# Seven products for the second part of layer 0's feed-forward network, with sums of weights made in DRAM during the convolutions

## The chip, the core and the metric

The kernel runs on one core of a Trainium2 chip, in one launch. The metric is the device time of one execution in microseconds; "before" and "after" are medians of several runs, and beside them stands one profiled execution of each kernel, from whose trace all views are taken.

## The reference

Two layers of a hybrid decoder over 512 tokens of width 1024, all in float32. Layer 0 is a Conformer convolution module and a SwiGLU feed-forward network, layer 1 sliding-window attention and another SwiGLU network. Cut to what matters here:

```python
def swiglu_ffn(x, w_up, w_down):              # w_up 1024 x 5632, w_down 2816 x 1024
    gate, up = jnp.split(x @ w_up, 2, axis=-1)
    return (jax.nn.silu(gate) * up) @ w_down

for l in range(2):
    if l == 0:   # causal depthwise convolution, 31 taps, per channel
        h = h + conformer_conv(rmsnorm(h, norm_mix[0]), ...)
    else:
        h = h + attention(rmsnorm(h, norm_mix[1]), k_shared, v_shared, ...) @ w_o
    h = h + swiglu_ffn(rmsnorm(h, norm_ffn[l]), ffn_w_up[l], ffn_w_down[l])
return rmsnorm(h, norm_final)
```

## The kernel before

Activations lie transposed, channels on the 128 partitions and tokens along the row. Products keep float32 accuracy by splitting each operand into a high and a low part of the faster float32r kind: a product is then three matmuls, high x high, high x low and low x high (`mm3`, L349 to L351). The high part of a weight chunk is a ScalarE copy (`whi`, L263), the low part a VectorE subtraction (`wlo`, L266). In the first products of layer 0 plain float32 is used instead (L347), with chunks that are not split.

Weights come in chunks of 128 x 1024 float32 (512 KB), in the fixed order of a list, `PLAN`. SyncE loads each into a `raw` buffer (L239, seven buffers, at most nine chunks ahead of use), and it is split at most three ahead of use. A buffer is free again when its split is done.

The hidden width of a feed-forward network is cut into eleven pairs of 256 columns of gate and 256 of up. **Layer 0's network** runs in two parts: pairs 0 to 4 (first part) separately for the two halves of the tokens, as each half leaves the convolution module, and pairs 5 to 10 (second part) for all 512 tokens at once. In the first part the second half's products use a form with two matmuls (`twin`, L381, L382). In the second part each pair takes four up chunks of 8 blocks of 128 x 128, each a `mm3` over 512 tokens; VectorE, ScalarE and GpSimd then form silu(gate) * up (L634 to L637), which is split for the down projection.

**Layer 1's network** takes ten of its eleven pairs by *seven products*: a pair's up weights and the rows x are cut into 2 x 2 blocks, and the four blocks of the result come from seven block products of 256 tokens (A11 B11, S1 T1, S2 T2, A12 B21, S3 T3, S4 B22, A22 T4) in place of eight. S1 to S4 are sums of weight blocks, T1 to T4 sums of blocks of rows. Its down projections go the same way ("low", L844). The results are gathered by ScalarE and VectorE (L784 to L796) and gated (L802 to L804, the last on GpSimd). T1 to T4 are made by GpSimd (L726) and split.

**The sums of weights** are made in DRAM, one chunk each, by `prepare` (60 of them): SyncE copies one block to a place in DRAM (L255), and GpSimd issues a transfer that adds another block onto it (L259). A sum that builds on another waits for that one to land, and what stands behind it in GpSimd's queue waits too. `share` says how many of these steps are taken per chunk used: 1/3 in the first part of the second token half, 1/2 in layer 0's second part, then 1, then 1/3.

**The convolution module** also works in two halves of 256 tokens. Its 31 taps per channel are divided: VectorE does some (L951), for the rest ScalarE multiplies (L943) and GpSimd adds (L944), and GpSimd adds both shares into `y` (L955). From y follow squares and sums (L1000), mean and variance, a spread over partitions (L1031), `z` (L1045), and the second projection on TensorE (L347). The taps of half 1 run beside the projections of half 0. The reciprocal root `rs` of the next norm is a GpSimd instruction (L474), and its spread (L496) stands in TensorE's queue among the first pairs' products.

In between SyncE and TensorE make a table for the attention bias: a small product at L1101, written 128 times over to DRAM (`fd`, 3 MB, L1104), read back in parts as bias tiles (L1195).

A scheduler orders each engine's instructions within the program's dependences; every engine works through its own list in that order. `issue_after` ties an instruction behind another one.

## Time and profile before

| | before |
|---|---|
| median of 3 runs | 1062.3 us (1059.25 to 1062.88) |
| the profiled execution | 1060.15 us |
| its span in the profile | 1058.4 us |
| TensorE's clock as granted, mean | 0.996 |
| TensorE busy | 1046.2 us, 99% of the span |
| VectorE, ScalarE, GpSimd busy | 737.6, 576.6, 437.8 us |
| moved by DMA | 211.04 MB |

All times in views are microseconds from the span's start, unless marked ns. Matmuls are pipelined, so "busy" of TensorE (PE) is not TensorE at its peak, and the mean duration of a matmul is longer than the distance from one to the next. PEld is its weight load, DVE is VectorE, ACT ScalarE, POOL GpSimd, SP SyncE. L259 is line 259 of the kernel before. "idle before <- X" is how long an engine stood idle ahead of a group and what ended that.

### The profile page before, as it was taken

To read this page: it belongs to the slowest core of one execution; us is meant where nothing else is said; L and a number is where in the kernel's file an instruction comes from. 1 tells how busy PE (TensorE), PEld (TensorE's weight loads), DVE (VectorE), ACT (ScalarE), POOL (GpSimd) and SP (SyncE) were. 2 spreads that over 40 slices of the span, in tenths; PEclk is the share of its full clock that TensorE was granted. 3 is DMA by queue.
4 is the path that set the end of the run, shared out by engine and by line. 5 is a ranking of instruction groups with operands and counts; after the bars stand their busy time and mean duration, and the time that the engine had idled before them with its cause. 6 is when DMAs were issued, how large, how long until landed. Compare 5 with 4: busy or idle time off the path is not lost.

```text
span 1058.4 us, 16667 instructions
## 1 busy us (share of the span) xinstructions
PE 1046.2 (99%) x6166; PEld 923.3 (87%) x6166; DVE 737.6 (70%) x1163; ACT 576.6 (54%) x1008; POOL 437.8 (41%) x535
## 2 busy tenths in 40 slices
PE   9999999999999999999999999999999999999996
PEld 8888889999988888888888877778989999898995
DVE  3999988977866654454427466678678777868677
ACT  3887897854645423322325465556655555554653
POOL 3999999810333312221124255305242323323131
PEclk9999999999999999999999999999999999999998
DMA  9438045577999996767779876765799565555532
GB/s 354 153 96 98 7 140 199 182 225 218 278 291 293 327 256 183 213 164 192 204 210 247 239 199 172 187 164 170 239 274 305 185 196 174 170 194 183 195 121 80
DMA packets 56606, 211.04 MB, mean 199 GB/s; under 512 B 6891, under 2 KB 13196, under 8 KB 55564
## 3 DMA queue, kind: packets, MB, share of 16 engines
q1 hardware_dynamic: 47164, 177.42, 49.8%
q0 software_dynamic: 8640, 31.46, 16.9%
q8 instruction: 48, 0.79, 0.3%
q10 hardware_dynamic: 720, 1.10, 0.3%
q14 instruction: 34, 0.28, 0.1%
HBM read 204.71 MB, written 68.16 MB: 258 GB/s over the span
## 4 chain that ended last, share of the span: by engine, by line
PE 89%; ACT 4%; issue 2%; POOL 2%; DVE 1%; DMA 1%; SPq 0%; ACTq 0%; POOLq 0%
PE bank L349 19%; PE bank L351 19%; PE bank L350 19%; PE bank L844 9%; PE bank L902 8%; PE bank L381 5%; PE bank L382 3%; ACT pr L943 1%; PE bank L1302 1%; PE bank L1344 1%; PE bank L1331 1%; PE bank L1000 1%; DMA sum<-in_W_dram 1%; POOL pr L944 1%; DMA both<-in_lead_dram 1%
## 5 line engine op out<-in xcount | busy, mean ns | idle before, releaser
L266 DVE TENSOR_TENSOR wlo<-raw,whi 128x1024 fp32r<-128x1024 f32 x231 | 305.8, 1332 | 166.1 <-ACT whi L263 165.1
L263 ACT CAST whi<-raw 128x1024 fp32r<-128x1024 f32 x231 | 241.2, 1049 | 274.8 <-PE bank L350 194.4
L349 PE MATMUL bank<-quad,whi 128*128 128x256 f32 (+1 forms) x976 | 326.9, 336 | 0.0
L350 PE MATMUL bank<-quad,whi 128*128 128x256 f32 (+1 forms) x976 | 326.0, 334 | 0.0
L351 PE MATMUL bank<-quad,wlo 128*128 128x256 f32 (+1 forms) x976 | 326.0, 334 | 0.0
L349 PEld LDWEIGHTS bank<-quad,whi 128*128 128x128 f32 x976 | 185.3, 190 | 19.8 <-issue 1.6
L351 PEld LDWEIGHTS bank<-quad,wlo 128*128 128x128 f32 x976 | 185.3, 190 | 18.8 <-issue 0.6
L350 PEld LDWEIGHTS bank<-quad,whi 128*128 128x128 f32 x976 | 185.4, 190 | 18.4 <-issue 0.2
L944 POOL TENSOR_TENSOR pr<-pr,pr 128x256 f32<-128x256 f32 x208 | 159.0, 798 | 3.8 <-ACT pr L943 3.8
L951 DVE SCALAR_TENSOR_TENSOR bank<-apad,wdw,bank 128x256 f32<-128x256 f32 x248 | 112.3, 484 | 3.3
L943 ACT ACTIVATE pr<-apad,wdw 128x256 f32<-128x256 f32 x208 | 98.2, 501 | 15.4 <-POOL pr L944 13.2
L804 POOL TENSOR_TENSOR up<-up 128x512 f32<-128x512 f32 x20 | 35.4, 1769 | 162.2 <-ACT up L803 162.2
L902 PE MATMUL bank<-quad,w 128*128 128x256 f32 x448 | 98.7, 380 | 0.0
L259 POOL DMA_DIRECT2D sum<-in_W_dram x30 | 25.0, 832 | 174.1 <-DMA sum<-in_W_dram 152.4
L902 PEld LDWEIGHTS bank<-quad,w 128*128 128x128 f32 x448 | 84.9, 190 | 11.8 <-DVE bank L951 0.2
L349 PE MATMUL bank<-rows,whi 128*128 128x256 f32 x320 | 90.8, 284 | 0.5 <-ACT up L788 0.5
L351 PE MATMUL bank<-rows,wlo 128*128 128x256 f32 x320 | 90.6, 283 | 0.0
L350 PE MATMUL bank<-rows,whi 128*128 128x256 f32 x320 | 90.5, 283 | 0.0
L259 POOL DMA_DIRECT2D sum<-sum x30 | 24.7, 823 | 140.7 <-DMA sum<-in_W_dram 128.4
L381 PE MATMUL bank<-quad,whi 128*128 128x512 f32 x212 | 76.0, 398 | 0.0
L349 PEld LDWEIGHTS bank<-rows,whi 128*128 128x128 f32 x320 | 61.4, 192 | 0.9 <-ACT up L788 0.7
L350 PEld LDWEIGHTS bank<-rows,whi 128*128 128x128 f32 x320 | 61.4, 192 | 0.3
(218 smaller groups left out, 1642.9 us busy)
## 6 DMA issues: line engine op xcount, KB each, us to landing
raw<-in_W_dram SPq DMA_DIRECT2D x183, 512.0 KB, 4.2
sum<-in_W_dram SPq DMA_DIRECT2D x60, 512.0 KB, 5.8
raw<-sum SPq DMA_DIRECT2D x60, 512.0 KB, 4.4
sum<-in_W_dram POOLq DMA_DIRECT2D x30, 512.0 KB, 7.0
sum<-sum POOLq DMA_DIRECT2D x30, 512.0 KB, 7.5
w<-in_W_dram SPq DMA_DIRECT2D x14, 512.0 KB, 9.3
fd<-fs SPq DMA_DIRECT2D x1, 3072.0 KB
h<-in_xT_dram SPq DMA_DIRECT2D x8, 256.0 KB, 8.4
```

The costliest lines, as they stand in the source:

```text
L259: nc.gpsimd.dma_start(summed[a], chunk(a, SUMS[a[2]][1]), accum_op=ALU.add, max_dma_last_dim=4096)
L263: on_act = nc.scalar.copy(hi, src).ins
L266: latest[:] = [on_act, lo_engine[0].tensor_sub(lo, src, f32(hi)).ins]
L349: nc.tensor.matmul(out, w[0], x[0], start=start, stop=False, **kw)
L350: nc.tensor.matmul(out, w[0], x[1], start=False, stop=False, **kw)
L351: nc.tensor.matmul(out, w[1], x[0], start=False, stop=stop, **kw)
L381: nc.tensor.matmul(first[2], first[0], first[1], start=start, stop=False)
L844: nc.tensor.matmul(out, x, w[:, ws], start=first and e == 0 and i == 0, stop=e == 1 and i == 2, skip_group_check=True)
L902: mm = nc.tensor.matmul(self.pb[:, w * W2:(w + 1) * W2], w1_of(ct, w, k), x[k] if x else xg[k][:, tok], start=k == 0, stop=k == KT - 1)
L943: on_act = nc.scalar.mul(pr, a[:, j:j + W2], tap(j))
L944: on_pool = nc.gpsimd.tensor_add(pr, acc, pr)
L951: on_dve = nc.vector.scalar_tensor_tensor(yt if i == nd - 1 else c, src, tap(i), c if i else self.shift, op0=ALU.mult, op1=ALU.add)
```

## The change

The six pairs of layer 0's second part (5 to 10) take their up projections by seven products too, from x and bc0 of both halves. The rows' sums T1 to T4 are made from the unsplit rows (`plain` of the first half, and a new `plain1` of the second), by GpSimd, in the first part of the second token half. `seven_pair` serves both layers now; for layer 0 it also multiplies the up half by the norm's factor, and writes into a pool of five buffers (`z0`), whose other tiles are `plain1` and T1 to T3. The down projections of the second part keep their matmuls and come after the six pairs.

The 24 sums of layer 0's pairs (S1 to S4 of six pairs) are made in four batches of six chunks, 3 MB each. The four copies are issued by SyncE behind the loads of the bias table's inputs. The four adds are issued by GpSimd: S1, S3 and S2 tied behind an add of the convolution's half 0, S4 behind one of half 1. Each add is one transfer of 768 rows of 4 KB. S2 adds onto A11 what S1 holds, S4 onto A12 what S2 holds.

Besides, the raw buffers go from seven to six, the first three bias tiles are read behind the six pairs instead of ahead of the first part, and `share` is 1/5 in the six pairs, then 1/2 in their down projections.

```diff
+EARLY_ADDS = {8: "S1", 9: "S3", 13: "S2"}
 def by_seven(layer, pair):
-    return layer == 1 and pair in SEVENS
+    return pair in SEVENS if layer else pair >= HALVES0[1][0]
...
-            r = wpool.tile([P, 1024], F32, tag="raw", name=uid("raw"), bufs=7)
+            r = wpool.tile([P, 1024], F32, tag="raw", name=uid("raw"), bufs=6)
...
+    def blocks_early(name):
+        if name[0] == "S":
+            return early_sums[name]
+        i = CHUNK_AT[EARLY[0] + (name,)]
+        return W[i:i + len(EARLY)].rearrange("u p c -> p u c")
+
+    def copy_early(name):
+        early_sums[name] = dpool.tile([P, len(EARLY), 1024], F32, tag=uid("sum"), name=uid("sum"))
+        for i, u in enumerate(EARLY):
+            summed[u + (name,)] = early_sums[name][:, i]
+        return nc.sync.dma_start(early_sums[name], blocks_early(SUMS[name][0])).ins
+
+    def add_early(name):
+        nc.gpsimd.dma_start(early_sums[name], blocks_early(SUMS[name][1]), accum_op=ALU.add, max_dma_last_dim=4096)
...
         def table_in():
             nc.sync.dma_start(sk, sinks.to_broadcast([P, NH]))
             nc.sync.dma_start(lhs[0:NBUCKET, :], relb)
-            nc.sync.dma_start(oh, onehot)
+            behind = nc.sync.dma_start(oh, onehot).ins
+            for name in ("S1", "S3", "S2", "S4"):
+                with tc.issue_after(behind):
+                    behind = copy_early(name)
...
+            if at_ in EARLY_ADDS:
+                with tc.issue_after(h0.pooled):
+                    add_early(EARLY_ADDS[at_])
...
         job(second, (base, 0), (base + 8, 19), (base + 13, 22), (base + 25, 40), (base + 36, h1.n_steps - early))
+        with tc.issue_after(h1.pooled):
+            add_early("S4")
...
-    def seven_pair(pair, rows, pool, between=None):
-        c = new_gates(pool)
+    def seven_pair(kind, pair, rows, c, between=None):
...
             nc.scalar.activation(gate, gate, AF.Silu)
+            if kind == "up0":
+                nc.vector.tensor_mul(c[:, m, :, 1, :], c[:, m, :, 1, :], rs_bc)
             nc.gpsimd.tensor_mul(gate, gate, c[:, m, :, 1, :])
...
+    class Rows0:
+        def sums(self):
+            b11, b12, b21, b22 = (f[:, j * 4:j * 4 + 4] for j in range(2) for f in self.f)
+            t1 = wpool.tile([P, 4, 256], F32, tag="raw", name=uid("t1"), bufs=6)
+            for n, (name, t, f, a, b) in enumerate((
+                    ("T1", t1, nc.gpsimd.tensor_sub, b11, b12), ("T2", b11, nc.gpsimd.tensor_add, b22, t1),
+                    ("T3", b12, nc.gpsimd.tensor_sub, b22, b12), ("T4", b21, nc.gpsimd.tensor_sub, b11, b21))):
+                f(t, a, b)
+                yield
+                ...
+                split([both[:, e] for e in range(2)], t, name == "T2")
+                yield
...
-    n1 = Next(("ffn0",), x0, bc0, HALF[1])
+    n1 = Next(("ffn0",), x0, bc0, HALF[1], plain=plain1)
+    job(rows0.sums(), (base + 10, 0), (base + 30, 9))
     pw2(h1.z, n1)
     ffn_part(0, 0, x0["ffn0"], HALF[1], n1.rms, twin=True)
...
+    share[0] = 1 / 5
+    lo0, hi0 = HALVES0[1]
+    hid0 = Act(2 * (hi0 - lo0))
+    for pair in range(lo0, hi0):
+        c = seven_pair("up0", pair, rows0, z0.tile([P, 2, 2, 2, 256], F32, tag="z0", name=uid("up"), bufs=5))
+        for m in range(2):
+            split([d.rearrange("p (s q) -> p s q", s=2) for d in hid0[2 * (pair - lo0) + m]], c[:, m, :, 0, :])
...
-        ffn_part(0, 1, x0["ffn0"], ALL, Both(), nxt.on_h)
+        for g in range(2):
+            banks = accs(512)
+            down_group([(("down", 0, kp, g), 2 * (kp - lo0)) for kp in range(lo0, hi0)], lambda kt: hid0[kt], banks)
```

More of the change, by code (lines that the diff above doesn't have):

```diff
@@ L87, in ffn @@
         for pair in range(lo, hi):
-            plan.extend(ups(layer, pair))
+            plan.extend(blocks_of("up0", pair) if by_seven(layer, pair) else ups(layer, pair))
         for g in range(2):
@@ L243, in prepare @@
     def prepare():
-        units = [c[:2] for c in PLAN if is_block(c) and c[2] == "S1"]
+        units = UNITS[len(EARLY):]
         adds, todo, before = [], [], None
@@ L391, in hybrid_trunk @@
     w1 = [None] + [quads.tile([P, 2, KT, P], F32, tag="quad", name=uid("w1")) for _ in range(1, KT)]
-    both = [wpool.tile([P, 1024], F32, tag="raw", name=uid("both"), bufs=7) for _ in range(KT // 2)]
+    both = [wpool.tile([P, 1024], F32, tag="raw", name=uid("both"), bufs=6) for _ in range(KT // 2)]
     x_first = [both[k // 2][:, k % 2 * 512:k % 2 * 512 + 256] for k in range(KT)]
@@ L728, in sums @@
                 both = quads.tile([P, 2, 4, 256], F32R, tag="quad", name=uid("rows"))
-                self.block[name] = [both[:, a] for a in range(2)]
-                split(self.block[name], t, name == "T2")
+                self.block[name] = [[both[:, e, k] for k in range(4)] for e in range(2)]
+                split([both[:, e] for e in range(2)], t, name == "T2")
     def new_gates(pool):
@@ L771, in seven_pair @@
         for n, name in enumerate(SEVEN):
[L772 removed]
+            w = [x.rearrange("p (a k c) -> p a k c", a=2, k=4) for x in get_seven(kind, pair, n)]
             a, b = name.split()
@@ L780, in seven_pair @@
                 for k in range(4):
-                    mm3(r[:, which], [v[:, which, k, :] for v in w], [x[e][:, k, :] for e in range(2)],
+                    mm3(r[:, which], [v[:, which, k, :] for v in w], [x[e][k] for e in range(2)],
                         first and which == 0 and k == 0, which == 1 and k == 3, skip_group_check=True)
@@ L1197, in read_bias, with __init__, step2 @@
                                       ap=[[NH * 3 * P - 1, P], [3 * P, 2], [1, BAND]]))
+    preparing[0], share[0] = prepare(), 1 / 3
+    class Rows0:
+        rms = None
+        def __init__(self, x, h0_, h1_):
+            self.f = h0_, h1_
+            self.block = {f"B{j + 1}{s + 1}": [[x[j * 4 + k][e][:, HALF[s]] for k in range(4)] for e in range(2)]
+                          for j in range(2) for s in range(2)}
+        def step2(self):
+            return bc0
+        def sums(self):
[6 more added lines that the diff above has]
+                yield
+                if n < 3:
+                    both = z0.tile([P, 2, 4, 256], F32R, tag="z0", name=uid("rows"), bufs=5)
+                else:
+                    both = quads.tile([P, 2, 4, 256], F32R, tag="quad", name=uid("rows"))
+                self.block[name] = [[both[:, e, k] for k in range(4)] for e in range(2)]
+                split([both[:, e] for e in range(2)], t, name == "T2")
+                yield
@@ L1199, in hybrid_trunk @@
+    part2 = ExitStack()
+    z0 = part2.enter_context(tc.tile_pool(name="part2", bufs=5))
+    plain1 = z0.tile([P, KT, W2], F32, tag="z0", name=uid("plain1"), bufs=5)
+    n1 = Next(("ffn0",), x0, bc0, HALF[1], plain=plain1)
     base = seen[0]
-    job(chain(*(read_bias(*b) for b in ((0, 0), (0, 1), (1, 0)))), (base, 0), (base + 30, 7))
-    preparing[0], share[0] = prepare(), 1 / 3
-    n1 = Next(("ffn0",), x0, bc0, HALF[1])
+    rows0 = Rows0(x0["ffn0"], plain, plain1)
+    rows0.rms = rows0
```

31 lines of the change are left out of this document (18 added, 13 removed).

## The prediction

> **What bounds the kernel now.** I read the page first (busy shares, the slices, the queues), then TensorE's waits, the windows and the timelines of single engines around the stages that the change touches. A page row gives busy us, share and instructions; a slice is 26.5 us, a digit tenths busy.
>
> ```profile
> span 1058.4 us, 16667 instructions
> ...
> PE 1046.2 (99%) x6166; PEld 923.3 (87%) x6166; DVE 737.6 (70%) x1163; ACT 576.6 (54%) x1008; POOL 437.8 (41%) x535
> ...
> POOL 3999999810333312221124255305242323323131
> DMA  9438045577999996767779876765799565555532
> ```
>
> TensorE waits for nothing worth naming: these are all its waits (us in total, times, longest).
>
> ```profile
> PE bank L434 <- POOL ones_m L431: 1.1, 1, 1.1
> PE bank L890 <- DVE quad L864: 0.9, 2, 0.6
> PE bank L349 <- ACT up L788: 0.5, 1, 0.5
> PE bank L496 <- ACT tmp L482: 0.2, 1, 0.2
> ```
>
> So matmul time taken out shortens the span, unless something makes TensorE wait. GpSimd is idle over most of the span, but not in the convolutions: slices 2 to 7 read 9. The fourth wait, at 179.6 us, is where its lateness reaches TensorE. DMA has room in slices 2 and 3 (4 and 3 tenths) and 5 (none busy).
>
> **What is saved.** Before, a pair of the second part is 4 chunks x 8 blocks x 3 = 96 matmuls of 512 columns; after, 7 products x 8 blocks x 3 = 168 of 256. The first two rows below are the same step of the first and the last pair (five pitches apart), the last two the same step of two neighbouring seven-product pairs of layer 1 (start, duration, instruction).
>
> ```profile
> 381.46 0.69 DVE L636 TENSOR_TENSOR tmp<-bank,rsbc 128x512 f32<-128x512 f32 x1 [0.59 <-PE bank L351]
> 490.26 0.69 DVE L636 TENSOR_TENSOR tmp<-bank,rsbc 128x512 f32<-128x512 f32 x1 [0.59 <-PE bank L351]
> 865.53 0.59 ACT L786 ACTIVATE up<-bank 128x512 f32<-128x512 f32 x1
> 885.69 0.59 ACT L786 ACTIVATE up<-bank 128x512 f32<-128x512 f32 x1
> ```
>
> (490.26 - 381.46) / 5 = 21.76 us now, 885.69 - 865.53 = 20.16 us by seven: 1.60 us a pair, less than the eighth of the columns that goes (a matmul of 256 takes 20.16 / 168 = 0.120 us). Six pairs: **9.6 us saved**. The down projections keep their matmuls.
>
> **What it costs in the stage itself.** Windows give us, then busy (instructions) of PE, PEld, DVE, ACT, POOL, granted clock, DMA share, GB/s; groups give busy us and mean ns.
>
> ```profile
> 290.00:345.00 55.00, 55.00 (x313) 47.55 (x312) 35.92 (x41) 29.06 (x47) 19.78 (x15) 1.00 0.94 290
> 450.00:500.00 50.00, 50.00 (x222) 41.43 (x221) 23.81 (x25) 15.41 (x19) 11.39 (x10) 1.00 0.67 181
> 830.00:890.00 60.00, 60.00 (x425) 56.41 (x424) 44.87 (x50) 32.58 (x42) 17.32 (x14) 1.00 0.57 186
> L266 DVE TENSOR_TENSOR wlo<-raw,whi 128x1024 fp32r<-128x1024 f32 x231 | 305.8, 1332 | 166.1 <-ACT whi L263 165.1
> L263 ACT CAST whi<-raw 128x1024 fp32r<-128x1024 f32 x231 | 241.2, 1049 | 274.8 <-PE bank L350 194.4
> L726 POOL TENSOR_TENSOR quad<-quad,quad x2: 3386/3388/3390, 722.4 to 725.7; 128x1024 f32<-128x1024 f32 x2
> L259 POOL DMA_DIRECT2D sum<-in_W_dram x30: 805/826/1040, 258.7 to 800.9; - x30
> 1015.75 5.52 PE bank L844 x24
> ```
>
> Seven chunks to split a pair are 7 x 1.33 = 9.3 us of VectorE and 7.3 us of ScalarE in 20.2; with evictions and gates some 16 and 13. Layer 1 runs so at 45 of 60 us: hidden; uncovered, 1.33 us a chunk. The four sums of rows (4 x 3.4 us of GpSimd, 4 x 1.05 of ScalarE, 4 x 1.33 of VectorE) and the second half's plain rows (eight ScalarE multiplies) lie in the part before, under TensorE, with 20, 29 and 36 busy of 55: hidden; uncovered, the first T1 product would wait 3.4 us per sum. One raw buffer fewer leaves six, 17 us ahead at 2.9 us a chunk: nothing, and 2.9 us where it ever fails. Layer 1's own sums fall behind by 36/2 - (42/5 + 12/2) = 3.6 of 60; at one in three chunks later on that is 31 us, and the last first-step add is issued at 801 us, the last low products start at 1016: nothing. The bias reads move to the down projections, where DMA was 0.67 busy: nothing.
>
> **What it costs in the convolutions.** The program's order shows four batch copies of 3 MB on SyncE behind the one-hot table and ahead of the first raw loads, and four batch adds on GpSimd's queue: S1 behind the 23rd of the 31 tap adds in the first row below, S3 twelve instructions on, S2 seven after that, S4 sixty behind S2.
>
> ```profile
> 70.11 21.31 POOL L944 TENSOR_TENSOR pr<-pr,pr 128x256 f32<-128x256 f32 x31
> ...
> 103.72 1.41 POOL L955 TENSOR_TENSOR y<-y,pr 128x256 f32<-128x256 f32 x2
> ...
> 178.13 0.71 POOL L474 TENSOR_TENSOR rs<-ms,mhalf 128x2 f32<-128x2 f32 x1
> ...
> 189.83 10.43 POOL L944 TENSOR_TENSOR pr<-pr,pr 128x256 f32<-128x256 f32 x9 [0.61 <-ACT pr L943]
> 110.00:180.00 70.00, 69.75 (x350) 61.71 (x348) 61.91 (x139) 58.30 (x133) 67.85 (x89) 1.00 0.35 121
> 179.62 0.70 PE L496 MATMUL bank<-tmp,ones_m 128*128 128x256 f32 x2 [0.25 <-ACT tmp L482]
> 129.41 1.89 PE L347 MATMUL bank<-z,raw 128*128 128x256 f32 x8
> ```
>
> GpSimd does one such add per 21.31 / 31 = 0.687 us without a gap. S1's turn is 23 adds behind 70.11, at 85.9 us; S3's comes 8.2 us after it, S2's 4.8 us after that, at 98.9 us plus two issues. S2 reads what S1 wrote and so waits for S1's landing. Behind it stand in line: the last two y of half 0 (103.72), on which the statistics, z and the second projection (129.41) hang; all taps of half 1; and the rs at 178.13, whose spread TensorE awaits at 179.62. GpSimd is 67.85 of 70 us busy up to there: what is put in ahead of rs is not made up. Slack: the order puts the spread 18 matmuls later (18 x 0.12 = 2.2 us) and one tap add behind rs (0.7), less the 0.25 waited already: 2.6 us. After 200 us GpSimd is free.
>
> How long is an issue, and when does S1 land?
>
> ```profile
> DMA to landing us min/median/max: 5.1/7.3/9.9
> ...
> q1 hardware_dynamic: 47164, 177.42, 49.8%
> q0 software_dynamic: 8640, 31.46, 16.9%
> 31.56 40.03 SPq L239 DMA_DIRECT2D raw<-in_W_dram  x7
> 73.91 0.34 SPq L1104 DMA_DIRECT2D fd<-fs  x1
> 78.00:82.00 4.00, 4.00 (x20) 3.52 (x19) 4.00 (x11) 3.30 (x8) 4.00 (x7) 1.00 0.89 101
> 102.00:106.00 4.00, 4.00 (x20) 3.54 (x19) 3.09 (x8) 3.55 (x10) 4.00 (x7) 1.00 0.90 100
> 106.00:110.00 4.00, 4.00 (x21) 3.51 (x20) 3.75 (x8) 1.92 (x4) 4.00 (x7) 1.00 0.26 38
> ```
>
> An issue d: 0.83 us for 128 rows (L259, above; min, median and max in ns); a batch has 768. It lies between 0.83 (all fixed) and 6 x 0.83 = 5.0 us (all per row); below 0.83 nothing points. I take 1.5, near the only row there is. The Trainium skill (DMA: Bandwidth & Descriptors, section Anatomy of one DMA) says that many descriptors can be emitted before their number costs; by that d would be 0.83 and the sum below come out 2.0 us lower; no run here shows a large batch.
>
> Copies: q1 moved 177.42 MB in 49.8% of 1058.4 us, 2.97 us per MB, so a 3.15 MB copy takes 9.3 us and four 37: from 32-36 to about 73 us, in DMA's hole. Raw loads wait behind them and are needed at 129: nothing; without that cover, 9.3 us each.
>
> The adds: q0 spent 16.9% of 1058.4 us on 60 adds of 512 KB, 2.98 us each; a batch takes 17.9 us of all engines. But the bias table's write (fd, issued at 73.91) holds 0.89 of the engines until 107 us. Alone S1 would land at 85.9 + d + 17.9 = 105; stretched as the small adds are, 7.3/5.1 = 1.43 times, at 113; at 9.9/5.1 = 1.94 times, at 122. I take 113. S2 lands behind S3, 2 x 17.9 us later, at 149 us; S4's turn is sixty instructions behind S2, 41 us, at 156: no wait.
>
> The sum: S2's turn is at 98.9 + 3.0 = 101.9, it waits 11.1 us; with four issues of 1.5, GpSimd is 17.1 us later at rs; less 2.6, TensorE loses 14.5. 14.5 - 9.6 = **+4.9 us**. On the profiled execution, 1060.15 us (span 1058.4), that is 1065.0; it lay 2.15 us below the median of 1062.3, so I forecast **1067 us**. Bounds of this case: d and landing from (0.83, 110) to (5.0, 118) give delays of 12.8 to 29 us less 2.6, so 1063 to 1079, its middle 1064 to 1073.
>
> **The rivals.**
>
> *S1 lands in time.* If the engines serve the add beside the slow table write, it lands at 104.6 with d = 0.83: the wait is 4.1, the delay 7.4, the loss 4.8, so 4.8 us faster, **1057**; with d = 2, where S2 waits 2.9 us, 1061. For it: the table write moves only 100 GB/s, so its share may be waiting, not moving. Against: 0.89 busy. The case turns to a gain where the delay stays under 12.2 us. Not waiting at all it gives 1053 at d = 0.83.
>
> *GpSimd is held while it issues.* The kernel gives these queues 2048 bytes per partition. If S3's descriptors don't fit beside S1's, GpSimd stands until most of S1 has drained, and S2's until most of S3, another 12 to 18 us: a delay of about 32 us, +20, **1082**. It decides as soon as two batches fill the ring; the small adds before never did. The Trainium skill (Perfetto Trace Analysis, section DMA Instruction — SWDGE (GPSIMD)) says engines begin before the last descriptor is written, the more so where they don't fit in the buffer. No row here shows a full one.
>
> *The seven products don't run at layer 1's pace.* GpSimd's sum adds stand in the same queue as the gates:
>
> ```profile
> POOL sum L259 <- DMA sum<-in_W_dram: 280.8, 48, 31.5
> ```
>
> If such a wait (31.5 us at worst) outlasts the two gate buffers, about 20 us, a pair stalls. Once, on top of the forecast, that is 11 us: **1078**. Against: layer 1 has the same queue and TensorE waited 0.5 us in it.
>
> **How the numbers follow.** The forecast 0.50, S1 in time 0.28, the full ring 0.13, slow products 0.09. A difference under 0.3% (3.2 us) can't be told from none. Faster by more, below 1059.1: about two thirds of S1 in time and a sliver of the forecast's smaller delays, 0.24. Same: the rest of S1 in time and the forecast's lower end, 0.16. Slower: 0.60. The range takes in S1 in time from 1055 and the upper cases up to 1081.
>
> **What would show it.** In the profile after: pair pitch 20.2 us from the first seven-product pair on; a wait of GpSimd at the S2 add for the S1 landing, about 11 us, ending near 113; y of half 0 some 10 to 12 us late; TensorE idle 11 to 15 us in all between 105 and 200 us, none of it later; the four issues 0.8 to 5 us each. Wrong it is if the S2 add finds S1 landed, if GpSimd stands at S3, or if TensorE stalls after 350 us.

## The result: slower by 5%, and the profile after

| | before | changed |
|---|---|---|
| median of the runs beside each other, us | 1062.59 (4 runs, 1059.25 to 1063.28) | 1116.08 (4 runs, 1112.93 to 1121.17) |
| ratio to before, 95% interval | | 1.0514 [1.0469, 1.0560] |
| span of the profiled execution, us | 1058.4 | 1111.1 |

The forecast was 1067 us in a range of 1055 to 1081. The sign was right, the size was not: the change costs 53 us. First the page of the changed kernel (busy us and share, then the 40 slices, 27.8 us each).

```profile
span 1111.1 us, 17707 instructions
...
PE 1044.5 (94%) x6598; PEld 939.1 (85%) x6598; DVE 781.2 (70%) x1203; ACT 615.3 (55%) x1062; POOL 454.2 (41%) x543
...
POOL 3994279794028331222212335522335342314132
PEclk9999579999998999999999999999999999999999
DMA  9999873955588999888997876766689985555542
```

TensorE's busy time is even a little shorter; its idle time grew from 12.2 to 66.6 us. GpSimd, full in slices 2 to 7 before, now has a hole in slices 4 and 5 (digits 4 and 2); TensorE's clock is down in slices 5 and 6 (5 and 7), and the DMA engines read 9 in slices 1 to 4. TensorE's waits say where that arrives (us in total, times, longest):

```profile
PE bank L1024 <- POOL y L979: 40.5, 3, 38.9
PE bank L517 <- ACT tmp L503: 7.0, 2, 3.8
PE bank L913 <- DVE quad L887: 1.9, 2, 1.6
PE bank L403 <- DVE wlo L287: 1.8, 2, 1.0
PE bank L372 <- DVE wlo L287: 1.7, 1, 1.7
```

One wait of 38.9 us for half 0's y, and two of 3 to 4 us at the spreads. GpSimd's own timeline (start, duration, instruction; in brackets the idle time before it and what ended that, "issue" meaning that nothing in the profile did) shows why y is late. L281 is the batch add, in the order S1, S3, S2.

```profile
70.26 15.82 POOL L967 TENSOR_TENSOR pr<-pr,pr 128x256 f32<-128x256 f32 x23
98.31 1.49 POOL L281 DMA_DIRECT2D sum<-in_W_dram  x1 [12.23 <-issue]
...
126.39 1.32 POOL L281 DMA_DIRECT2D sum<-in_W_dram  x1 [18.37 <-issue]
...
146.25 1.17 POOL L281 DMA_DIRECT2D sum<-sum  x1 [13.75 <-issue]
...
149.72 1.16 POOL L979 TENSOR_TENSOR y<-y,pr 128x256 f32<-128x256 f32 x1
...
229.84 1.72 POOL L495 TENSOR_TENSOR rs<-ms,mhalf 128x2 f32<-128x2 f32 x1
```

An issue itself takes 1.2 to 1.5 us, but GpSimd stands 12.2, 18.4 and 13.8 us in front of three of them: 44.4 us. With the four issues (5.2 us) that is 49.6 of the 51.7 us by which rs is late (178.13 before). The first data packet of S1 is at 107.8 us, and each batch then moves for 16 to 18 us: S1 to 125.8, S3 128.5 to 145.6, S2 148.1 to 164.2. GpSimd is let go at S3 and at S2 just when the batch before has drained. These windows (us, then busy of PE, PEld, DVE, ACT, POOL, granted clock, DMA share, GB/s) show what the engines did meanwhile, and the price of standing still:

```profile
86.00:98.00 12.00, 12.00 (x57) 10.58 (x56) 3.06 (x8) 0.51 (x1) 0.08 (x1) 1.00 0.89 98
98.00:108.00 10.00, 8.47 (x38) 6.62 (x38) 6.15 (x14) 6.23 (x14) 9.69 (x13) 1.00 0.89 97
114.00:154.00 40.00, 4.42 (x10) 3.36 (x11) 6.17 (x14) 8.81 (x19) 13.86 (x20) 0.50 0.84 160
343.00:349.00 6.00, 4.65 (x13) 3.89 (x14) 6.00 (x7) 3.70 (x9) 6.00 (x3) 0.50 0.67 207
```

In the first two the table's write is all that moves, at 97 to 98 GB/s, also after S1 has been issued. In the last two the granted clock is 0.50: after these stalls TensorE first ran on at half speed, 5 us of it behind the long one.

The saving is there. The same step of two seven-product pairs of layer 0, four pitches apart:

```profile
452.10 0.59 ACT L807 ACTIVATE up<-bank 128x512 f32<-128x512 f32 x1
532.27 0.59 ACT L807 ACTIVATE up<-bank 128x512 f32<-128x512 f32 x1
```

(532.27 - 452.10) / 4 = 20.04 us a pair, against 21.76 before and 20.16 forecast. By TensorE's marks the 52.7 us of the span come about so, to within half a microsecond: the spread of half 0 is at 232.3 in place of 179.6 (+52.7), the last twin matmul at 422.9 in place of 361.9 (another +8.3), the first attention matmul at 651.8 in place of 598.7 (7.9 back). Two questions, then: what holds GpSimd, and what takes 8 us of the twin part (the first part's second half of the tokens), which I had taken to hide the new work.

### The profile page after: what moved, and what is told of

Its sections match the earlier page's. It is cut to its first block, busy times and chain, and to the rows that moved or that the text cites. A ratio compares the mean times of both kernels' runs of the same rounds, so it can differ in the third digit from the quotient of the medians.

```text
span 1111.1 us, 17707 instructions
## 1 busy us (share of the span) xinstructions
PE 1044.5 (94%) x6598; PEld 939.1 (85%) x6598; DVE 781.2 (70%) x1203; ACT 615.3 (55%) x1062; POOL 454.2 (41%) x543
## 4 chain that ended last, share of the span: by engine, by line
PE 71%; issue 8%; DVE 7%; POOL 7%; ACT 3%; DMA 2%; SPq 0%; DVEq 0%; POOLq 0%; ACTq 0%
PE bank L370 18%; PE bank L372 18%; PE bank L371 18%; PE bank L867 9%; POOL pr L967 4%; DVE bank L975 3%; DMA sum<-in_W_dram 2%; DVE wlo L287 1%; PE bank L402 1%; PE bank L1376 1%; PE bank L1418 1%; PE bank L1405 1%; ACT pr L966 1%; DVE quad L525 1%; PE bank L403 1%
## 5 line engine op out<-in xcount | busy, mean ns | idle before, releaser
L287 DVE TENSOR_TENSOR wlo<-raw,whi 128x1024 fp32r<-128x1024 f32 x249 | 337.3, 1364 | 127.7 <-ACT whi L284 126.0
L284 ACT CAST whi<-raw 128x1024 fp32r<-128x1024 f32 x249 | 259.6, 1048 | 274.0 <-PE bank L371 191.5
L372 PE MATMUL bank<-quad,wlo 128*128 128x256 f32 (+1 forms) x928 | 292.4, 316 | 1.7 <-DVE wlo L287 1.7
L370 PE MATMUL bank<-quad,whi 128*128 128x256 f32 (+1 forms) x928 | 293.0, 317 | 0.0
L371 PE MATMUL bank<-quad,whi 128*128 128x256 f32 (+1 forms) x928 | 292.3, 315 | 0.0
L370 PEld LDWEIGHTS bank<-quad,whi 128*128 128x128 f32 x928 | 177.3, 191 | 12.2 <-issue 1.3
L371 PEld LDWEIGHTS bank<-quad,whi 128*128 128x128 f32 x928 | 177.4, 191 | 10.9 <-issue 0.2
L370 PE MATMUL bank<-rows,whi 128*128 128x256 f32 x512 | 144.7, 283 | 0.0
L371 PE MATMUL bank<-rows,whi 128*128 128x256 f32 x512 | 144.6, 283 | 0.0
L372 PE MATMUL bank<-rows,wlo 128*128 128x256 f32 x512 | 144.4, 282 | 0.0
L827 POOL TENSOR_TENSOR up<-up 128x512 f32<-128x512 f32 x32 | 55.3, 1727 | 192.2 <-ACT up L824 192.2
L371 PEld LDWEIGHTS bank<-rows,whi 128*128 128x128 f32 x512 | 97.7, 191 | 0.3
L370 PEld LDWEIGHTS bank<-rows,whi 128*128 128x128 f32 x512 | 97.7, 191 | 0.3
L372 PEld LDWEIGHTS bank<-rows,wlo 128*128 128x128 f32 x512 | 97.6, 191 | 0.0
L925 PEld LDWEIGHTS bank<-quad,w 128*128 128x128 f32 x448 | 85.6, 192 | 12.2 <-DVE bank L975 0.2
```

The lines of the kernel that those rows point to most:

```text
L284: on_act = nc.scalar.copy(hi, src).ins
L287: latest[:] = [on_act, lo_engine[0].tensor_sub(lo, src, f32(hi)).ins]
L370: nc.tensor.matmul(out, w[0], x[0], start=start, stop=False, **kw)
L371: nc.tensor.matmul(out, w[0], x[1], start=False, stop=False, **kw)
L372: nc.tensor.matmul(out, w[1], x[0], start=False, stop=stop, **kw)
L827: nc.gpsimd.tensor_mul(gate, gate, c[:, m, :, 1, :])
```

## The experiments

| run | median us (runs) | ratio to before [95%] |
|---|---|---|
| ring4096 | 1099.17 (4) | 1.0342 [1.0311, 1.0373] |
| six_adds | 1109.80 (4) | 1.0436 [1.0404, 1.0469] |
| spaced | 1072.41 (4) | 1.0104 [1.0059, 1.0150] |
| fd_late | 1116.39 (4) | 1.0513 [1.0475, 1.0550] |
| fd_behind | 1116.35 (4) | 1.0529 [1.0510, 1.0547] |
| no_adds | 1064.28 (10) | 1.0026 [1.0004, 1.0047] |
| no_adds_t_later | 1065.70 (10) | 1.0030 [1.0012, 1.0049] |
| no_adds_rows_later | 1062.41 (10) | 1.0014 [0.9998, 1.0030] |
| rows_on_vector | 1055.44 (4) | 0.9932 [0.9906, 0.9958] |
| share_up | 1060.69 (10) | 0.9986 [0.9963, 1.0009] |
| raw6 | 1061.95 (10) | 1.0000 [0.9983, 1.0017] |
| behind_rs | 1069.08 (10) | 1.0052 [1.0028, 1.0076] |
| one_early | 1065.91 (6) | 1.0044 [1.0027, 1.0062] |
| none_early | 1084.86 (4) | 1.0232 [1.0212, 1.0252] |
| best1 | 1057.80 (6) | 0.9949 [0.9932, 0.9967] |
| best2 | 1061.29 (12) | 0.9988 [0.9972, 1.0005] |

### What holds GpSimd

**ring4096** gives the software queue twice the memory.

```diff
-    ... dynamic_dma_scratch_size=2048)
+    ... dynamic_dma_scratch_size=4096)
```

> Only the software queue's scratch memory is changed, from 2048 to 4096 bytes a partition. Theory R (GpSimd is held at a batch because the queue's ring has no room for a second batch's descriptors): the hold of 18.4 us at S3 goes, the hold of 12.2 us at S1 shrinks or goes, GpSimd then waits for S1 to land before S2 (S1's data 107.8 to 125.8 us), so some 15 to 25 us come back: 1091 to 1101 us. Theory E (GpSimd is held because the 16 DMA engines are full, whatever the ring): no change, 1113 to 1119 us, with the holds of 12, 18 and 14 us where they were.

Measured: 17 us faster than the changed kernel, inside the span that theory R gave. GpSimd's batch adds:

```profile
98.95 1.49 POOL L281 DMA_DIRECT2D sum<-in_W_dram  x1 [12.65 <-issue]
108.11 1.81 POOL L281 DMA_DIRECT2D sum<-in_W_dram  x1
126.76 1.19 POOL L281 DMA_DIRECT2D sum<-sum  x1 [12.03 <-DMA sum<-in_W_dram]
```

The hold of 18.4 us at S3 is gone, and the one at S2 has become a wait for a named landing, S1's: the prediction's own mechanism. So the holds at S3 and S2 are the full ring. The hold at S1, where the ring is empty (nothing went out on that queue before), stayed, against what theory R said of it: that one is something else.

**six_adds** issues each batch as six adds of 128 rows at the same place.

```diff
-        nc.gpsimd.dma_start(early_sums[name], ...)
+        for i in range(len(EARLY)):
+            nc.gpsimd.dma_start(early_sums[name][:, i], ...)
```

> Each batch add is issued as six adds of 128 rows at the same place. Theory R: the ring holds a few adds of 128 rows, GpSimd is held when it is full, so the hold shrinks by what fits but does not go: S3's last adds are held until S1's have mostly drained; 1095 to 1115 us, with the issues' own time up from 4 x 1.3 to 24 x 0.6 to 0.8 us. Theory E: the same as one batch, or slower by the added 10 us of issues, 1116 to 1130 us. If a batch's size itself were the trouble (no second transfer of 768 rows at once), it would come down to 1070 us.

Measured, inside theory R's span: S1's six go out together behind the same hold of 12.25 us, S3's first without a hold, and each of S3's other five stands 1.4 to 2.2 us until some of the ring has drained; with four short holds in S2 that is 26.2 us in all. The ring holds one batch and one small add, then, and not two batches. An add of 128 rows that stands alone takes 0.81 to 0.87 us, so the batch's 1.2 to 1.5 us are mostly a fixed cost.

**fd_late** was to move the table's write (fd) out of S1's way.

```diff
-            nc.sync.dma_start(fd..., fs...)      # in table()
+        nc.sync.dma_start(fd..., fs...)          # behind pw2(h0.z, n0)
```

> The write of the bias table (fd, 1536-byte rows, 79 to 110 us in the kernel as changed) is moved behind the first loads of layer 0's weights, so that it is no longer in flight when S1 is issued; nothing else is changed. Theory F (GpSimd is held 12.2 us at S1, ring empty, because the engines are full of the table's rows): the hold at S1 goes (under 2 us), S1's data start within 1 us of its issue, at about 87 us, and not 8 us behind it; the holds at S3 and S2 stay as waits for the batch before to drain, 8 to 12 us each, so the wait of TensorE's bank at y falls from 38.9 to 15 to 25 us and the time to 1085 to 1100 us. Rival (the first batch of GpSimd's queue is held for a reason of its own, such as its first use): the hold at S1 stays at 10 to 13 us and the time at 1110 us and over.

It didn't move: SyncE had nothing to wait for ahead of it and issued it at 73.67 us (74.04 in the changed kernel), so the run repeats the changed kernel and says nothing of the cause.

**fd_behind** ties it to a raw load that waits for TensorE, so that it is issued at 174.3 us.

```diff
+        def table_out():
+            yield
+            with tc.issue_after(loaded[0]):
+                nc.sync.dma_start(fd..., fs...)
+            yield
+        job(table_out(), (base + 2, 0), (base + 3, 2))
```

> The step that fd_late was meant to be: the table's write is now put on SP's queue behind loads that wait for TensorE (the last before it waits at about 130 us), so that it is not in flight while S1 is issued at 86 us. Theory F (engines full of the table's 1536-byte rows hold GpSimd): hold at S1 under 2 us, S1's first data at about 87 us in place of 107.8, holds at S3 and S2 of 8 to 12 us each, TensorE's longest wait at y 15 to 25 us in place of 38.9. Rival (the first batch of the software queue is held for a reason of its own): hold at S1 10 to 13 us, first data at 106 to 108 us, wait at y 35 us and over. The time itself also carries the table's write falling among the weight loads, so it is not the measure here: 1080 to 1115 us by the theory.

```profile
85.19 1.20 POOL L281 DMA_DIRECT2D sum<-in_W_dram  x1
106.32 1.32 POOL L281 DMA_DIRECT2D sum<-in_W_dram  x1 [11.68 <-issue]
126.20 1.17 POOL L281 DMA_DIRECT2D sum<-sum  x1 [13.77 <-issue]
```

S1 goes out in its turn, with its first data at 87.1 us, 0.7 us after the issue's end. TensorE's longest wait at y is 21.8 us in place of 38.9. So it is the table's write that held GpSimd at S1, with an empty ring, and put S1's data off: in the changed kernel 113 of its 2048 rows of 1536 bytes were left when S1's first packet came. The time, 1116 us, is just over the theory's span: the 17 us won at y are lost again where the write now stands among the weight loads (one wait of 20.2 us for a raw load).

How the write does it is not shown, and theory F's words for it, engines full of rows, go further than the traces. Later in fd_behind S4 was in flight when the write came, and from 183 to 189 us the two queues went turn about, row for row (packets, MB, share of the engines):

```profile
q0 software_dynamic: 248, 1.02, 84.6%
q1 hardware_dynamic: 247, 0.38, 20.4%
```

The write moved 63 GB/s there with a share of 0.20; alone it showed 0.89 at 97 GB/s. A busy engine in that row is thus not an engine without room. A rival that no run separates: in each of the four traces with the hold at S1, GpSimd is let go 1.7 us after the start of an 8 KB packet on a queue that the profile calls "instruction", here from 96.5 to 97.0 us of the changed kernel:

```profile
q14 instruction: 1, 0.01, 3.9%
```

These packets start at 96.1 to 97.2 us; in fd_behind the one in that place starts at 83.2, ahead of S1's turn, and in the kernel before, which has the write but no batch, at 97.1. The write delays this packet, then, whether or not a batch is issued, and GpSimd may have waited for it and not for its descriptors.

**spaced** keeps ring and table and moves the four adds into half 1's taps, behind the table's write.

```diff
-EARLY_ADDS = {8: "S1", 9: "S3", 13: "S2"}
+EARLY_AT = {14: 'S1', 38: 'S3', 62: 'S2', 86: 'S4'}   # count of half 1's tap adds
```

> The four batch adds are moved into half 1's taps, at 14, 38, 62 and 86 adds of half 1, so that they are issued at about 109, 128, 147 and 166 us, behind the table write and some 19 us apart. Both theories (ring empty, engines free at each issue): no hold over 3 us, four issues of 1.2 to 1.5 us, y of half 0 as in the kernel before, TensorE's idle of 38.9 us at the bank gone: 1055 to 1066 us. If a hold stays although fd is written and the batch before has landed, GpSimd is held by the batch's own transfer: 1100 us and over.

Measured: S1 at 109.6 without a hold, S3 at 130.0 with 0.8, S2 at 155.3 with 4.8, just behind S3's last packet at 154.4 (S3 drained beside the raw loads); 44 of the 54 us are gone. What is left is over the forecast: rs at 195.2, 17 us late. Part of that does not come from a hold: one VectorE operation, 0.41 us as a rule, took 11.31 us, to the end of a run of GpSimd adds without a gap (156.0 to 167.3 us).

```profile
154.85 0.41 DVE L481 TENSOR_TENSOR tmp<-tmp,tmp 128x256 f32<-128x256 f32 x1
156.29 11.31 DVE L481 TENSOR_TENSOR tmp<-tmp,tmp 128x256 f32<-128x256 f32 x1
```

ScalarE's next products came late behind it, and GpSimd then idled 9.2 us for them. The twin part shows the same between the two engines, below.

### What the rest is worth

**no_adds** leaves the four adds out and keeps everything else. It and the four runs built on it (no_adds_t_later, no_adds_rows_later, rows_on_vector, share_up) give another result than the reference: they price parts of the change and are no kernels to use.

```diff
-        nc.gpsimd.dma_start(early_sums[name], ..., accum_op=ALU.add, ...)
+        pass
```

> The four batch adds are left out: the sums of weights of layer 0 are only copies of their first addend, so the output is another. Everything else, the seven products and the copies among it, stays. Theory: nearly all of the loss of 53 us before the first spread of layer 0 is GpSimd's holds at the batches; without them the convolution ends as in the kernel before, and what is left is the gain of part 2 (7.9 us in the trace) less the loss ahead of it that has nothing to do with the batches (T1 ahead of rs with the half-clock stretch behind it, up to 8 us): 1054 to 1063 us. Rival (the copies, and fd beside them, cost the convolution too): over 1070 us.

1064.3 us, just over the forecast: the adds cost 52 us, and without them the change is still not faster than the kernel before. Part 2 gains 9.9 us in this trace (last twin matmul to first attention 226.9 us against 236.8), but the twin part loses 7.3 us, and layer 1's low products take 269.1 us against 261.7. Five runs take that apart.

**no_adds_t_later** starts the rows' sums four steps later, so that T1 stands behind rs.

```diff
-    job(rows0.sums(), (base + 10, 0), (base + 30, 9))
+    job(rows0.sums(), (base + 14, 0), (base + 30, 9))
```

> As no_adds (the four batch adds left out, so the sums of layer 0 are only copies of their first addend), and the sums of rows T1 to T4 begin four steps later, so that T1 stands behind rs in GpSimd's order. Theory: of the 7.3 us that no_adds loses against the kernel before between the half-0 spread and the last twin matmul, 3.7 are the wait at the spread behind T1 and some 3.4 the half-granted clock after it; both go, and the kernel shows the seven products' gain: 1054 to 1058 us. Rival (the wait at the spread is rs's own or comes from ScalarE): 1062 to 1066 us as in no_adds.

A miss: the wait at the spread is only down from 3.7 to 2.3 us, and the time is unchanged. **no_adds_rows_later** also takes the plain rows out of ScalarE's chain to the spread, and T1 to T4 start behind them.

```diff
-    n1 = Next(("ffn0",), x0, bc0, HALF[1], plain=plain1)
+    n1 = Next(("ffn0",), x0, bc0, HALF[1])
...
+            for i in range(KT):
+                with tc.issue_after(n1.rms.on_act):
+                    nc.scalar.mul(plain1[:, i, :], h[i][:, HALF[1]], col("ffn0", i))
```

> As no_adds (the four batch adds left out, so the sums of layer 0 are only copies of their first addend), with the plain rows of half 1 (8 products of 0.5 us on ScalarE) and T1 to T4 moved behind the diagonal of half 1's scale. Theory: the plain rows stand in ScalarE's chain from pw2 to the half-1 spread and cost the 2.3 to 3.7 us wait there and the half clock behind it; moved, TensorE reaches its last twin matmul 4 to 7 us sooner than in no_adds: 1056 to 1060 us. Rival (the four splits of T rows on ScalarE and VectorE are what makes the weights late in that stage, wherever they start): 1063 to 1067 us, with the waits on wlo as they were.

The wait at the spread falls to 1.1 us and the half-clock stretch behind it is gone, but the stage is as long as ever: 4.9 us of waits on wlo have come in, and the 1062.4 us measured lie between the two forecasts, nearer to the rival's. TensorE's marks of the twin part, before and here (count, ns, first and last start):

```profile
L381 PE MATMUL bank<-quad,whi x212: 387/397/579, 276.6 to 361.5; 128*128 128x512 f32 x106
```

```profile
L402 PE MATMUL bank<-quad,whi x212: 387/397/583, 276.4 to 370.0; 128*128 128x512 f32 x106
```

84.9 us against 93.6. In that trace VectorE and GpSimd, around the sums:

```profile
318.84 6.73 DVE L287 TENSOR_TENSOR wlo<-raw,whi 128x1024 fp32r<-128x1024 f32 x2
325.49 3.43 DVE L533 TENSOR_TENSOR rows<-t,rows 128x1024 fp32r<-128x1024 f32 x1
```

```profile
318.35 2.79 POOL L1254 TENSOR_TENSOR t<-plain,plain 128x1024 f32<-128x1024 f32 x1 [0.28 <-DVE wlo L287]
321.22 3.27 POOL L1254 TENSOR_TENSOR plain<-plain,t 128x1024 f32<-128x1024 f32 x1
324.45 6.72 POOL L1254 TENSOR_TENSOR plain<-plain 128x1024 f32<-128x1024 f32 x2
```

Two splits that take 1.2 us each when alone take 3.4, and each ends 1.08 us behind the end of a GpSimd sum. **rows_on_vector** makes the sums on VectorE.

```diff
-                    ("T1", t1, nc.gpsimd.tensor_sub, b11, b12), ...
+                    ("T1", t1, nc.vector.tensor_sub, b11, b12), ...
```

> As no_adds_rows_later (the four batch adds left out, so the sums of layer 0 are only copies of their first addend), with T1 to T4 on VectorE in place of GpSimd. Theory P (GpSimd's sums over 128 x 1024, two operands in SBUF, hold VectorE's splits of weights, 5 us of the waits on wlo in that stage): VectorE takes on four sums of 1.3 us but its splits fall back from 3.4 us to 1.2 to 1.4 us, the waits on wlo in the stage fall from 4.9 us to under 2, the stage from 93.6 to 86 to 89 us: 1056 to 1060 us. Rival (VectorE is simply full in that stage): the waits stay or grow, 1062 to 1066 us.

Measured: 1055.4 us, 7 us faster than with the sums on GpSimd, and faster than before, though without the four adds.

```profile
317.40 1.23 DVE L1254 TENSOR_TENSOR t<-plain,plain 128x1024 f32<-128x1024 f32 x1
319.15 1.22 DVE L287 TENSOR_TENSOR wlo<-raw,whi 128x1024 fp32r<-128x1024 f32 x1
320.28 1.22 DVE L1254 TENSOR_TENSOR plain<-plain,t 128x1024 f32<-128x1024 f32 x1
```

```profile
L402 PE MATMUL bank<-quad,whi x212: 387/395/577, 276.1 to 362.6; 128*128 128x512 f32 x106
```

A sum is 1.23 us on VectorE against 2.8 to 3.4 on GpSimd, the splits between them are at 1.22 again, and the stage takes 86.5 us. Theory P holds: GpSimd's sums did not cost their own time, which was idle there, but VectorE's. The Trainium skill (SBUF — State Buffer, section SBUF: two separate sides) says that the two share a pair of SBUF ports under an exclusive lock, which a VectorE operation with two SBUF inputs and a GpSimd operation that reads SBUF contend for; these traces agree (1.22 us for a split alone, 6.73 us for two beside the sums).

**share_up** gives layer 1's sums a larger share in part 2.

```diff
-    share[0] = 1 / 5
+    share[0] = 2 / 5
```

> As no_adds_rows_later (batch adds left out, as there), with the share of layer 1's sums in part 2 raised from 1/5 to 2/5 a chunk, so that 8 more of them are made before the attention. Theory L (layer 1's sums come late and crowd its first 60 us, where DMA's share is 1.00 and 0.93 against 1.01 and 0.71 before and TensorE idles 4 us): the 4 us in layer 1's first three stretches go: 1057 to 1060 us. Rival (the idle there is chance of the trace, or part 2's weights come late instead): 1061 to 1066 us.

The first 30 us of layer 1's low products, before, in no_adds_rows_later and here:

```profile
776.80:806.80 30.00, 30.00 (x175) 26.46 (x174) 29.16 (x31) 17.33 (x21) 14.18 (x11) 1.00 1.01 307
```

```profile
775.70:805.70 30.00, 28.83 (x161) 24.88 (x160) 28.42 (x29) 16.02 (x20) 12.21 (x11) 1.00 1.00 313
```

```profile
777.70:807.70 30.00, 30.00 (x176) 26.46 (x175) 28.00 (x31) 17.27 (x21) 12.72 (x8) 1.00 0.63 202
```

DMA is down to 0.63, TensorE idles no more, and the low products take 261.6 us, as before, in place of 267.0. But the first attention is 1.8 us later, and between the two totals (1060.7 against 1062.4) the intervals overlap: shown for the stage, not for the whole.

**raw6** is the kernel before with six raw buffers.

> The kernel before with 6 raw buffers in place of 7, nothing else. The changed kernel gave one up for its rows. If a buffer less makes the weights late (new waits of TensorE on the weight splits in layer 1 in no_adds: 5 us with a half-clock stretch behind them): 1065 to 1070 us. If it is free, as I took it to be: 1060 to 1064 us.

No difference: in the kernel before the seventh buffer was free, as forecast. The changed kernel, which loads seven chunks a pair, was not run with seven.

### Where the adds can go

**behind_rs**: S1 and S3 in half 1's taps, S2 behind rs of half 0, S4 behind rr of half 1 (`rr` is the reciprocal root in the convolution module's norm), T1 behind rs.

```diff
+EARLY_AT = {14: 'S1', 38: 'S3', 96: 'S2'}
...
-    job(rows0.sums(), (base + 10, 0), (base + 30, 9))
+    job(rows0.sums(), (base + 14, 0), (base + 30, 9))
```

> S1 and S3 at 14 and 38 of half 1's adds as in spaced (about 110 and 130 us), S2 behind rs of half 0 and S4 behind rr of half 1, and T1 behind rs. Theory: only two issues (2.7 us) are left ahead of the half-0 spread, no hold over 3 us stands before it, VectorE's starved 11.3 us of spaced go with GpSimd's lag, and the spread behind T1 no longer waits: 1054 to 1060 us. If the adds behind rs take the DMA engines from the weight loads: new waits on the splits in layer 0's first part, 1062 to 1070 us.

1069.1 us, above the forecast. No hold was over 0.4 us, but two issues ahead of rs put it off to 180.9 (178.1 before) and the spread waited 3.6 us, and the sums still stood in the twin part on GpSimd. **one_early** leaves one issue ahead of rs (S1), puts S3 behind rs, S2 behind rr of half 1 and S4 behind T4, with the rows as in no_adds_rows_later. **none_early** puts all four behind rs (S1 behind rs, S3 behind rr, S2 behind T1, S4 behind T4).

```diff
-EARLY_AT = {14: 'S1', 96: 'S3'}     # one_early
+EARLY_AT = {96: 'S1'}               # none_early
```

> S1 at 14 of half 1's adds (about 109 us), S3 behind rs of half 0, S2 behind rr of half 1, S4 behind T4, and the plain rows and T sums as in no_adds_rows_later. One issue of 1.2 us stands ahead of the half-0 spread. Theory: no hold over 3 us, spread on time, and the row sums out of its way: within 3 us of no_adds_rows_later, 1056 to 1063 us. If the batches' 70 us of DMA engines behind rs make the weights late: waits on the weight splits in layer 0's first part, 1066 us and over.

> All four batch adds behind rs of half 0: S1 there, S3 behind rr of half 1, S2 behind T1, S4 behind T4; the rest as one_early. Nothing is left of the batches in the convolution ahead of rs. If an issue there costs its own 1.2 us: 0 to 3 us less than one_early, 1055 to 1062 us. If the adds then come too late for the first pair of seven products (S4 lands after 375 us) or crowd the weight loads: 1066 us and over.

one_early is at 1065.9 us, 3.5 us above no_adds_rows_later: just above the forecast's span, with waits of 9.2 us on wlo in all against 6.3. none_early is at 1084.9: S4 is issued at 345.4 us, having waited 7.6 us for S2's landing, and TensorE waits 18.6 us once on a split in the last twin products, in a stretch where the DMA engines are full (1.06 from 340 to 370 us). The trace shows the chain of that wait, and it is a hold again: behind S4 one add of layer 1 goes out, the next stands 25.58 us until S4 has nearly drained beside the weight loads, and behind it on GpSimd stands a product (L594) for which VectorE waits ahead of the split.

```profile
376.18 0.84 POOL L262 DMA_DIRECT2D sum<-sum  x1 [25.58 <-issue]
377.79 0.94 DVE L595 TENSOR_TENSOR h<-h,tmp 128x256 f32<-128x256 f32 x1 [20.30 <-POOL tmp L594]
```

one_early has such a hold of 10.85 us at 358.8. The issue in the convolution that none_early saves is worth nothing beside that.

**best1** is one_early with the sums on VectorE, the share at 2/5, and S4 behind rs of half 1.

> one_early with both edits: T1 to T4 on VectorE, share 2/5, and S4 behind rs of half 1. If theories P and L hold: 4 us each less than one_early's 1065.9: 1055 to 1060 us, faster than the kernel before. If neither: 1064 to 1068 us; if only one: 1060 to 1063 us, no difference to before.

1057.8 us, 0.9949 [0.9932, 0.9967] of the kernel before: the one version with the reference's result that is faster than both, by half a per cent over the kernel before. Against rows_on_vector, which has no adds, the twin part is still longer, 91.4 us against 86.5. Its window there:

```profile
320.00:350.00 30.00, 26.57 (x141) 21.14 (x140) 27.47 (x28) 17.98 (x27) 12.36 (x10) 1.00 1.00 313
```

I put that down to S4, issued at 290 us, whose transfers fill the engines beside the weight loads. GpSimd is also held behind S4 here, at the second add of layer 1 after it.

```profile
318.29 0.83 POOL L262 DMA_DIRECT2D sum<-sum  x1 [11.45 <-issue]
```

**best2** issues S4 straight behind S2.

```diff
-            with tc.issue_after(n1.rms.on_rs):
-                add_early("S4")
...
+                        behind = add_early("S2")
+                    with tc.issue_after(behind):
+                        add_early("S4")
```

> best1 with S4 issued straight behind S2 (GpSimd idles for 30 us there and waits for S2's landing at about 253 us), so that S4's transfers end at about 275 us, ahead of the half 1 stage. If S4 beside the weight loads of that stage is what best1 loses against rows_on_vector: the stage falls from 91.9 to 87 to 89 us, 1053 to 1056 us. If the larger share in part 2 or the crowding as a whole is: 1057 to 1060 us.

A miss: 1061.3 us. S4 now goes out at 252.7, the twin part takes 90.0 us in place of 91.4, but the crowding moved ahead: an add of layer 1 waits 11.1 us for its copy at 285.2, the last sums of squares of half 1's norm stand behind it on GpSimd, and TensorE waits 3.9 us for them. The hold of 11.45 us is gone, and yet the twin part is only 1.4 us shorter. So S4's place alone is not what best1 loses against rows_on_vector; how much of it is the larger share, and how much the batches as a whole, stays open.

## Why the prediction was wrong

**The saving**, 1.60 us a pair and 9.6 in all: right. 20.04 us a pair were measured, and part 2 gained 7.9 us in the changed kernel, 9.9 in no_adds and rows_on_vector.

**The issue**, d = 1.5 us: right, 1.17 to 1.49. The Trainium skill's rule weighed there (DMA: Bandwidth & Descriptors, section Anatomy of one DMA), that many descriptors go out before their number costs, agrees in the main: six times the rows added 0.3 to 0.7 us, where a cost by rows alone would have added some 4.

**The step that failed** is "S1 lands at 113, S2 waits 11.1 us", with GpSimd free until S2. It took a batch add for something that GpSimd hands over in its turn. GpSimd was held 12.2 us at S1, 18.4 at S3 and 13.8 at S2, and S2's turn came only when S1 had long landed. That S2 waits for S1 at all was sound, as ring4096 showed once the ring had room. That it waits 12.0 us there, near the 11.1 forecast, is luck: its turn came at 114.7 in place of 101.9 and S1's landing near 126.7 in place of 113, both some 13 us late. The 2.6 us of slack taken off did not show either: rs came 51.7 us late and its spread 52.7.

**The rival that held**, GpSimd held while issuing, had 0.13 and was priced at 1082. Its condition, two batches that don't fit, was met (ring4096, six_adds). The price fell short for three reasons. It gave the holds and issues about 32 us in all, where two drains follow one another (18.4 and 13.8 us) and the issues add 5.2; it took the ring to be the only reason to be held, where the table's write held S1 for 12.2 us as well and put its data off to 107.8 us (fd_behind); and the 8.3 us of the twin part were in no rival. The prediction stretched S1's landing by 1.43 for that write; measured, S1's 18 us of data came almost wholly behind it. The Trainium skill (DMA: Bandwidth & Descriptors, section Queues, rings and completion order) says that each engine takes turns between its queues packet by packet. In the changed kernel the write went on at 97 to 98 GB/s for 8 us with S1 issued and in line; in fd_behind, where S4 was moving first, the trace shows such turns, 248 packets against 247. So the two can share the engines, and why S1 had to wait for its first turn is left open. The Trainium skill's other rule quoted in the prediction (Perfetto Trace Analysis, section DMA Instruction — SWDGE (GPSIMD)), that data may start before the issue ends, no trace here bears out: they came 8 us after it in the changed kernel and 0.7 us after it in fd_behind.

**"Hidden" in the stage itself**: wrong, by 7 to 8 us. The sums were weighed by GpSimd's idle time in that window; they cost VectorE's time there (rows_on_vector, 7 us). T1 ahead of rs and the plain rows in ScalarE's chain made TensorE wait at the spread (3.7 us in no_adds, 2.3 with T1 later, 1.1 with both moved). Layer 1's sums that fall behind were put at nothing by their last one; it is the first 60 us of layer 1 that they crowd (share_up, 5.4 us in that stage). The raw buffer at nothing was right in the kernel before (raw6).

**The half clock** was in no term. Every stall of TensorE of 3.2 us or more in the middle of these traces had a stretch at a granted clock of 0.50 with it, of 3.4 or 6.8 us where the stall was under 5; of the shorter stalls some had one (2.1 us in fd_behind) and some had none (3.0 us in one_early). At the half-1 spread of no_adds TensorE was back at work at 292.1 us, behind a wait of 3.7, and ran at half speed to 296.9:

```profile
292.10:296.90 4.80, 4.80 (x14) 4.04 (x15) 4.80 (x6) 2.34 (x6) 4.80 (x2) 0.50 0.70 215
```

By that, as an estimate, the stall cost another 2.4 us. The Trainium skill (TensorE: Matmul & The Clock Gate, Part 1) gives an activity window of about 3.4 us, and full and half speed as the two states; the lengths of the stretches agree. It asks for an idle window of that length; here some stalls of 2.1 us were enough.

Of the three signs named as making it wrong, the two that matter came: S1 had landed when S2 was issued, and GpSimd stood at S3. The third, a stall of TensorE after 350 us, came to 1.0 and 1.7 us.

## What to carry to other kernels

Before a large transfer goes on GpSimd's queue, ask what is in flight on the DMA engines and whether the transfer before it has drained: in these runs GpSimd stood idle until then, and everything queued behind the issue was late with it, a small add behind a large one included. Work moved to an engine's idle time need not be hidden: price GpSimd's two-operand work on SBUF by what VectorE does meanwhile. And price a stall of a few us with the half-clock stretch that may follow.

## What the runs showed of the hardware

- GpSimd is held at a DMA issue by a full ring (18.4 us; gone with 4096 bytes) and also, with an empty one, while another queue's write of 1536-byte rows is in flight (12.2 to 13.0 us in four traces; gone with that write elsewhere). Whether it then waits for the DMA engines or for the packet on the "instruction" queue, 1.7 us ahead of its release in all four, is open.
- The queue's 2048 bytes hold one add of 768 rows and one of 128, and not two of 768; the next add of 128 rows behind these was held up to 25.58 us (none_early). 4096 bytes hold two of 768.
- Two queues with work go turn about on the engines, row for row (248 against 247 packets in 6 us of fd_behind), and the share that the profile gives a transfer is not what it needs: the same write showed 0.89 alone and 0.20 beside S4.
- A VectorE tensor_tensor with both operands in SBUF can starve beside back-to-back GpSimd adds: 11.31 us in place of 0.41 (spaced).
- TensorE's granted clock went to 0.50 behind some stalls as short as 2.1 us (fd_behind, 3.4 us long), and not behind one of 3.0 us (one_early).
